# Grouping the output products of a recurrence, and letting TensorE run empty at four weight tiles

## The chip, the cores and the metric

The kernel runs on one core of a Trainium2 chip. The metric is device time in microseconds (us) of one execution; the kernel before takes 1694.59 us, the median of three runs (1694.12 to 1694.8).

## The reference

The input is a sequence of 256 tokens of width 1024. It goes through two blocks. The first has four residual steps: an attention, a squared-ReLU MLP, a gated linear recurrence and another MLP. The second, on which the change acts, puts 16 learned tokens ahead and has one mixer and one expert layer:

```
z = rmsnorm(h, g_mix) @ w_in
conv_val, conv_gate, rwkv_in, gate_logits = jnp.split(z, IN_SPLITS, axis=-1)
y_a = conformer_conv(conv_val, conv_gate, ...)     # 31 taps per channel, 512 channels
y_b = rwkv7_mix(rwkv_in, ...)                      # 8 heads of 64, a state S of 64 x 64 each
h = h + (gate_a * y_a + gate_b * y_b) @ w_o
h = h + peer_ffn(rmsnorm(h, g_ffn), w_q, sub_keys, expert_u, expert_v)
return rmsnorm(h, g_final)[:, N_META:]
```

The recurrence of `rwkv7_mix` is, token by token, `sa = S kk`, `S = S * w - sa (kk * a) + v k`, `o = S r`. `peer_ffn` picks for each token and each of 8 heads 16 of 16384 experts (the best sums of two lists of 128 keys), and gives the sum of gate x GELU(x · u[e]) x v[e] over the 128 chosen experts e.

## The kernel before, in words

**Weights and products.** Every weight tile is 128x1024 in float32 (512 KB). The class `Stream` (L67) loads it on SyncE's queue (`wraw`, L98), ScalarE rounds it to fp32r (`whi`, L121) and VectorE subtracts that from it (`wlo`, L122). A product with such a weight is three products of 256 columns: high by high, high by low, low by high. `mm_T` (L387, products in L392 to L394) runs over the eight 128-row parts of a tile and adds up in one PSUM bank; `mm_blk` (L406, L412 to L414) runs the eight blocks of a tile into four banks, which `product` (L416) holds over all of its tiles. TensorE, shown as PE, takes its weights through a load of their own (PEld) ahead of each product.

**The recurrence.** The 272 tokens are cut into five chunks (c = 0 to 4), the first with the 16 learned tokens. `inverse(c)` (L1117) finds the inverse of a triangular 64x64 matrix per head in steps: VectorE transposes and masks, TensorE multiplies (`p`, `px`, through `mm_heads`, L1115: eight 64x64 products, four head pairs hp times the two halves e of the array, a half being 64 rows and 64 columns). `recur(c)` (L1171) then does the chunk: `pG` (L1175) from the state SV, `pSA` from the inverse X and G, SAV as a copy of it by ScalarE and VectorE (L1182, L1183), the next state through `pN` (L1189) and VectorE (L1194, L1195), and for c of 1 and above the chunk's output `po`: for every head pair and half a product of SV with PRB over all 128 rows (L1203) and, added to it, one of SAV with UC over the 64 rows of its half (L1205). ScalarE copies po into oT (L1207). The steps of the next two chunks' inverses are issued between the steps of `recur`. Beside it TensorE works off products of the input projection (`pz`, L916), and VectorE the 30 taps of the convolution (`cy`, L1230, 120 operations).

**The expert layer.** `peer` (L1344) computes the keys' scores, and then goes over 128 U tiles (L1557): one `mm_T` each into `pu`, the GELU by ScalarE (L1561), and to DRAM. In tiles 0 to 59 VectorE chooses the experts beside it (`select`, L1446; its steps are tied to the GELU of three tiles before), in 60 to 127 `gates` (L1520) builds the gates with short bf16 products on TensorE (`pG`, L1538). Then come 128 V tiles in one `product` (L1615): VectorE multiplies gate and activation (`c`, L1551), the result is split, and the products `yp` of L412 to L414 add up over all tiles; the last three are held back and finished bank by bank.

**Order.** The Tile framework's scheduler puts each engine's instructions in order by its own estimate of when they can start, from the order of the code and its dependences; `tc.issue_after` holds an instruction behind another. On each engine they then run in that order. PSUM tiles of `bank` (L223) rotate over four banks, those of `ybank` are named.

Of the kernel before, what the change touches and what calls it, by code (L numbers as in the profile page):

```python
# [2 lines left out]

# [1 line left out]

# [8 lines left out]
BF16 = mybir.dt.bfloat16  # L14
# [178 lines left out]
def fused_kernel(ctx, tc, A, out, dbg=None, stop=None, start2=False):  # L193
    nc = tc.nc
# [28 lines left out]
    def bank(name, shape=(128, 512)):  # L223
        return ps.tile(list(shape), F32, name=name, tag="g")
# [47 lines left out]
    st = Stream(nc, wraw_p, whl_p, tiles, ahead=2, raw_ahead=2, plain=PLAIN)  # L272
# [33 lines left out]
    TOK = slice(0, T)  # L306
# [80 lines left out]
    def mm_T(p, w, blk, nk, x_hi, x_lo, cs):  # L387

        hi, lo = w
        for k in range(nk):  # L390
            s = slice((blk * nk + k) * 128, (blk * nk + k + 1) * 128)
            nc.tensor.matmul(p, hi[:, s], x_hi[:, k, cs], start=(k == 0), stop=False)  # L392
            nc.tensor.matmul(p, hi[:, s], x_lo[:, k, cs], start=False, stop=False)  # L393
            nc.tensor.matmul(p, lo[:, s], x_hi[:, k, cs], start=False, stop=(k == nk - 1))  # L394

    def mm_T2(nk, x_hi, x_lo, cs, *pw):

# [8 lines left out]
    def mm_blk(ys, blk, w, a_hi, a_lo, first, last):  # L406

        hi, lo = w
        y = ys[blk // 2][:, blk % 2]
        s = slice(blk * 128, (blk + 1) * 128)  # L410
        kw = dict(skip_group_check=True)
        nc.tensor.matmul(y, hi[:, s], a_hi, start=(first and blk % 2 == 0), stop=False, **kw)  # L412
        nc.tensor.matmul(y, hi[:, s], a_lo, start=False, stop=False, **kw)  # L413
        nc.tensor.matmul(y, lo[:, s], a_hi, start=False, stop=last, **kw)  # L414

    def product(n, operand, finish, name, hold=3):  # L416


        ys = ybanks(name)
        held = []  # L420
        for k in range(n):
            if k == n - hold:
                st.pause(hold)
            w, a_hi, a_lo = operand(k)
            if k < n - hold:
                for blk in range(8):
                    mm_blk(ys, blk, w, a_hi, a_lo, k == 0, False)
            else:
                held.append((w, a_hi, a_lo))
        for b in range(4):  # L430
            for i, (w, a_hi, a_lo) in enumerate(held):
                for blk in (2 * b, 2 * b + 1):
                    mm_blk(ys, blk, w, a_hi, a_lo, n == hold and i == 0, i == hold - 1)
            last = finish(b, ys[b])
        return last
# [418 lines left out]
    def mixers(gg, h2, es, setup, after):  # L854
# [10 lines left out]
        with ExitStack() as e2:  # L865
            nk = pool(e2, "mx_n")
# [13 lines left out]
            for tt in range(2):  # L880
                nc.tensor.matmul(pcol[:, tt], row[:, tt * 128:(tt + 1) * 128], ident[0:2, 0:2],
                                 start=True, stop=True)
# [46 lines left out]
        cs = ap.tile([128, 4, 5, 65], F32, name="cs")  # L929
# [37 lines left out]
        for hp in range(4):  # L967
            s = slice(hp * 128, (hp + 1) * 128)
# [18 lines left out]
        PRB = [o2.tile([128, 5, 4, 2, 64], F32, name=f"PRB{e}") for e in range(2)]  # L987
# [28 lines left out]
        for hp in range(4):  # L1016
# [7 lines left out]
            for e in range(2):  # L1024
                r = slice(64 * e, 64 * e + 64)
# [5 lines left out]
        for hp in range(4):  # L1031
# [3 lines left out]
            for e in range(2):  # L1035
                r = slice(64 * e, 64 * e + 64)
# [18 lines left out]
        for j in range(4):  # L1055
            sgs = wk.tile([128, NT], F32, name="sgc", tag="zd")
            p = bank("pz", (128, NT))
            mm_F(p, 4 + j, ALLT)
            nc.scalar.activation(sgs, p, AF.Sigmoid)
            p = bank("pz", (128, NT))  # L1060
# [6 lines left out]
        for c in range(5):  # L1067
            pab = [ybank(e, f"pab{e}", (128, 4, 128)) for e in range(2)]
            for hp in range(4):
                for e in range(2):  # L1070
                    r = slice(64 * e, 64 * e + 64)
                    nc.tensor.matmul(pab[e][:, hp], QK[r, c, hp].rearrange("p a b -> p (a b)"),
                                     PRB[e][r, c, hp].rearrange("p a b -> p (a b)"),
                                     start=True, stop=True)
            for e in range(2):
                for half in range(2):
                    r = slice(64 * half, 64 * half + 64)
# [20 lines left out]
        SV = [bp.tile([128, 5, 4, 64], F32, name=f"SV{e}") for e in range(2)]  # L1098
# [7 lines left out]
        def rb(name, shape):  # L1106
            rot[0] += 1
            return ybank(rot[0] % 4, name, shape)

        HALF = [slice(0, 64), slice(64, 128)]  # L1110
# [60 lines left out]
        def recur(c):  # L1171
            pG = rb("pG", (128, 4, 64))
            for hp in range(4):
                for e in range(2):
                    nc.tensor.matmul(pG[HALF[e], hp], PRB[e][:, c, hp, 0, :], SV[e][:, c, hp],  # L1175
                                     start=True, stop=True)
            G = wk.tile([128, 4, 64], F32, name="G")
            nc.scalar.activation(G, pG, AF.Copy)
            yield
            pS = rb("pSA", (128, 4, 64))  # L1180
            mm_heads(pS, lambda r, hp: X[r, c, hp], lambda r, hp: G[r, hp])
            nc.scalar.activation(SAV[0][0:64, c], pS[0:64], AF.Copy)  # L1182
            nc.vector.tensor_copy(SAV[1][64:128, c], pS[64:128])  # L1183
            yield
            if c < 4:
                pN = rb("pN", (128, 4, 64))
                for hp in range(4):
                    for e in range(2):
                        nc.tensor.matmul(pN[HALF[e], hp], QN[:, c, hp, 64 * e:64 * e + 64],  # L1189
                                         SAV[e][:, c, hp], start=True, stop=True)  # L1190
                for e in range(2):
                    r = HALF[e]
                    t = wk.tile([128, 4, 64], F32, name="Sn")
                    nc.vector.tensor_tensor(t[r], SV[e][r, c], pN[r], op=ALU.add)  # L1194
                    nc.vector.tensor_tensor(SV[e][r, c + 1], t[r],  # L1195
                                            wc[r, :, c:c + 1].to_broadcast([64, 4, 64]),
                                            op=ALU.mult)
            if c >= 1:
                po = rb("po", (128, 4, 64))
                for hp in range(4):  # L1200
                    for e in range(2):
                        r = HALF[e]
                        nc.tensor.matmul(po[r, hp], SV[e][:, c, hp], PRB[e][:, c, hp, 1, :],  # L1203
                                         start=True, stop=False, skip_group_check=True)
                        nc.tensor.matmul(po[r, hp], SAV[e][r, c, hp], UC[r, c, hp, 1, :],  # L1205
                                         start=False, stop=True, skip_group_check=True)
                nc.scalar.activation(oT[:, :, (c - 1) * 64:c * 64], po, AF.Copy)  # L1207
            yield
# [10 lines left out]
        for c in range(5):  # L1219
# [3 lines left out]
            r = recur(c)  # L1223
# [23 lines left out]
        for tt in range(2):  # L1247
            for j in range(4):
                nc.tensor.matmul(pvr[:, 2 * tt:2 * tt + 2], sqc[:, j, tt * 128:(tt + 1) * 128],
                                 ones, start=(tt == 0 and j == 0), stop=(j == 3),  # L1250
                                 skip_group_check=True)
# [4 lines left out]
        for tt in range(2):  # L1256
            nc.tensor.matmul(prd[:, tt * 128:(tt + 1) * 128],
                             rsd[:, tt:tt + 1].to_broadcast([128, 128]), ident,
                             start=True, stop=True)
        nc.vector.tensor_tensor(cy, cy, prd[:, None, :].to_broadcast([128, 4, T]), op=ALU.mult)  # L1260
        a_hi = fp.tile([128, 4, T], F32R, name="a_hi")
        a_lo = fp.tile([128, 4, T], F32R, name="a_lo")
# [21 lines left out]
        for tt in range(2):  # L1284
            s = slice(tt * 128, (tt + 1) * 128)
# [23 lines left out]
        for b in range(16):  # L1309
            if b == GN_AT:  # L1310
                grouped()
            p = bank("pz", (128, T))
# [9 lines left out]
        for i in range(4):  # L1322
            w = st.get(("w_co", i))
            for b in range(2):
                p = bank("pya", (128, T))
                mm_T(p, w, b, 4, a_hi, a_lo, TOK)
                blk = 2 * i + b
                nc.vector.tensor_tensor(sm[:, blk], gates[:, blk], p, op=ALU.mult)
        for i in range(4):
            w = st.get(("w_ro", i))  # L1330
            for b in range(2):
                p = bank("pyb", (128, T))
                mm_T(p, w, b, 4, b_hi, b_lo, TOK)
                blk = 2 * i + b
# [3 lines left out]
        after = product(8, lambda k: (st.get(("w_o2", k)), s_hi[:, k], s_lo[:, k]),  # L1338
                        then_h(col("g_ffn", 0, 8), h2, REAL), "yw")
# [4 lines left out]
    def peer(h2, after):  # L1344
# [5 lines left out]
        rp = pool(es, "pe_r", side="right")  # L1350
# [6 lines left out]

        iorep = rp.tile([128, 128, 2], BF16, name="iorep")
        nc.vector.tensor_copy(iorep, iota[:, :, None].to_broadcast([128, 128, 2]))
        p_hi = rp.tile([128, DC, T], F32R, name="p_hi")  # L1360
        p_lo = rp.tile([128, DC, T], F32R, name="p_lo")

# [20 lines left out]
        for hc in range(18):  # L1383
            if hc < 16:
                if hc < 4:
                    p = pw[hc][0]
# [169 lines left out]
        acts = []  # L1556
        for i in range(128):  # L1557
            p = bank("pu", (128, T))
            mm_T(p, st.get(("u", i)), 0, 8, p_hi, p_lo, TOK)
            hs = h_out[(i // 2) % 4]  # L1560
            acts.append(nc.scalar.activation(hs[:, i % 2], p, AF.Gelu))  # L1561
            if i % 2:
                nc.scalar.dma_start(H[i // 2], hs)
            if ge is not None and c0 is None and next(ge, "done") == "done":
                eu.close()
                cw = pool(es, "pe_c", 3, side="right")
                c0 = combine(0)
            for _ in range(STEPS[i % len(STEPS)]):
                if ge is not None:
                    continue  # L1570
                if i >= U_LAG:
                    with tc.issue_after(acts[i - U_LAG].ins):
                        r = next(se, "done")
                else:
                    r = next(se, "done")
                if r == "done":
                    st.less(PE_MORE)
                    st.less_raw(PE_RAW)
                    ez.close()
                    eh.close()  # L1580
                    G = pool(es, "pe_l").tile([128, 128, T], F32, name="G")
                    ge = gates(G)
                    assert i == U_TOP
# [28 lines left out]
            if b >= 1:  # L1612
                add_sums(b - 1)

        product(128, operand, fin, "yp")  # L1615
        add_sums(3)
        ms = cw.tile([128, 2], F32, name="ms")
        nc.vector.tensor_scalar(ms, psum[:, 0:4:2], 1.0 / D, EPS, op0=ALU.mult, op1=ALU.add)
# [125 lines left out]
```

## Time and profile before

| | |
|---|---|
| median of three runs | 1694.59 us (1694.12 to 1694.8) |
| the profiled execution, its time | 1702.62 us |
| its span | 1700.9 us |
| TensorE products, busy | 1669.2 us (98% of the span) |
| VectorE busy | 1244.0 us (73%) |
| ScalarE busy | 861.3 us (51%) |
| GpSimd busy | 29.8 us (2%) |
| mean granted TensorE clock | 0.986 of full speed |

The span is the time from the first to the last instruction of the profiled execution. A busy TensorE means that products are in flight, not that they follow one another as closely as they can: products overlap, and so their mean duration is longer than the distance between their starts. The stages that matter here stand in this order in the span: the recurrence at about 690 to 778 us, the expert layer's U tiles at about 882 to 1318, its V tiles at about 1318 to 1682.

### The profile page before, as it was taken

How to read it: one execution, taken by the hardware profiler on the slowest of the kernel's cores; microseconds unless marked ns; L12 is line 12 of the kernel's file. 1: busy time of each engine (PE TensorE's matmuls, PEld its weight loads, DVE VectorE, ACT ScalarE, POOL GpSimd, SP SyncE). 2: the span in 40 equal slices, each digit the busy share in tenths (PEclk: the TensorE clock that was granted, in tenths of full speed). 3: DMA queues.
4: the chain of work that ended last, by engine and by line, in shares of the span. 5: the costliest groups of instructions: out<-in, count | busy, mean ns of one | idle time of the engine just before them, and what ended most of it. 6: DMA issues, size and time to landing. Idle time of an engine off the chain costs nothing.

```text
span 1700.9 us, 35211 instructions
## 1 busy us (share of the span) xinstructions
PE 1669.2 (98%) x14458; PEld 1598.2 (94%) x14458; DVE 1244.0 (73%) x2204; ACT 861.3 (51%) x1400; POOL 29.8 (2%) x76
## 2 busy tenths in 40 slices
PE   8999999999999999999999999999999999999997
PEld 7889999899999978778999999999999999999997
DVE  6767555889555688776789984977777777777774
ACT  7555545586544463214465445655555544444443
POOL 0000000011000000001000000000000000000000
PEclk9999999999999999899999999999999999999999
DMA  8426666446665223113664778555555877777773
GB/s 292 135 87 211 188 196 212 136 122 227 199 192 181 74 87 112 39 39 112 211 220 153 217 245 271 173 186 186 185 182 185 298 235 231 236 231 236 229 224 110
DMA packets 96227, 309.75 MB, mean 182 GB/s; under 512 B 12593, under 2 KB 12721, under 8 KB 95681
## 3 DMA queue, kind: packets, MB, share of 16 engines
q1 hardware_dynamic: 83808, 287.61, 53.5%
q10 hardware_dynamic: 11904, 18.25, 2.9%
q8 instruction: 113, 1.85, 0.4%
q0 software_dynamic: 352, 1.64, 0.3%
q14 instruction: 50, 0.40, 0.1%
HBM read 288.58 MB, written 18.87 MB: 181 GB/s over the span
## 4 chain that ended last, share of the span: by engine, by line
PE 87%; DVE 7%; ACT 2%; DMA 2%; issue 1%; POOL 0%; DVEq 0%; SPq 0%; POOLq 0%; ACTq 0%
PE pu L392 10%; PE pu L394 10%; PE pu L393 10%; PE yp L414 7%; PE yp L412 7%; PE yp L413 7%; PE pz L916 4%; PE ym L413 3%; PE ym L414 3%; PE ym L412 3%; PE pG L1538 3%; DVE wlo L122 2%; PE yv L495 1%; ACT whi L121 1%; DVE cy L1230 1%
## 5 line engine op out<-in xcount | busy, mean ns | idle before, releaser
L121 ACT ACTIVATE whi<-wraw 128x1024 fp32r<-128x1024 f32 (+1 forms) x501 | 520.5, 1042 | 549.3 <-PE yp L413 174.2
L122 DVE TENSOR_TENSOR wlo<-wraw,whi 128x1024 fp32r<-128x1024 f32 (+1 forms) x501 | 600.0, 1204 | 254.3 <-ACT whi L121 253.5
L392 PE MATMUL pu<-p_hi,whi 128*128 128x256 f32 x1024 | 292.3, 285 | 0.0
L413 PE MATMUL yp<-p_lo,whi 128*128 128x256 f32 x1024 | 287.8, 281 | 0.0
L412 PE MATMUL yp<-p_hi,whi 128*128 128x256 f32 x1024 | 287.8, 281 | 0.0
L414 PE MATMUL yp<-p_hi,wlo 128*128 128x256 f32 x1024 | 287.6, 281 | 0.1
L394 PE MATMUL pu<-p_hi,wlo 128*128 128x256 f32 x1024 | 286.6, 280 | 0.1
L393 PE MATMUL pu<-p_lo,whi 128*128 128x256 f32 x1024 | 286.7, 280 | 0.0
L413 PEld LDWEIGHTS yp<-p_lo,whi 128*128 128x128 f32 x1024 | 196.5, 192 | 0.0
L393 PEld LDWEIGHTS pu<-p_lo,whi 128*128 128x128 f32 x1024 | 194.5, 190 | 0.0
L394 PEld LDWEIGHTS pu<-p_hi,wlo 128*128 128x128 f32 x1024 | 193.2, 189 | 0.3 <-DVE wlo L122 0.3
L414 PEld LDWEIGHTS yp<-p_hi,wlo 128*128 128x128 f32 x1024 | 192.2, 188 | 0.3 <-DVE wlo L122 0.3
L392 PEld LDWEIGHTS pu<-p_hi,whi 128*128 128x128 f32 x1024 | 192.2, 188 | 0.2 <-ACT xT L1561 0.2
L412 PEld LDWEIGHTS yp<-p_hi,whi 128*128 128x128 f32 x1024 | 192.2, 188 | 0.0
L413 PE MATMUL ym<-s_lo,whi 128*128 128x256 f32 x512 | 142.3, 278 | 1.7 <-DVE s_lo L326 1.6
L412 PE MATMUL ym<-s_hi,whi 128*128 128x256 f32 x512 | 142.4, 278 | 0.5 <-ACT s_hi L325 0.5
L414 PE MATMUL ym<-s_hi,wlo 128*128 128x256 f32 x512 | 142.0, 277 | 0.0
L392 PE MATMUL pu<-h_hi,whi 128*128 128x256 f32 x480 | 133.6, 278 | 0.0
L394 PE MATMUL pu<-h_hi,wlo 128*128 128x256 f32 x480 | 133.2, 277 | 0.2 <-DVE wlo L122 0.2
L393 PE MATMUL pu<-h_lo,whi 128*128 128x256 f32 x480 | 133.1, 277 | 0.0
L413 PEld LDWEIGHTS ym<-s_lo,whi 128*128 128x128 f32 x512 | 96.7, 189 | 2.3 <-DVE s_lo L326 2.3
L412 PEld LDWEIGHTS ym<-s_hi,whi 128*128 128x128 f32 x512 | 96.1, 188 | 0.9 <-ACT s_hi L325 0.7
(479 smaller groups left out, 3317.0 us busy)
## 6 DMA issues: line engine op xcount, KB each, us to landing
wraw<-in_w_dram SPq DMA_DIRECT2D x128, 512.0 KB, 3.6
wraw<-in_u_dram SPq DMA_DIRECT2D x128, 512.0 KB, 3.5
wraw<-in_v_dram SPq DMA_DIRECT2D x128, 512.0 KB, 4.2
wraw<-in_w_in_dram SPq DMA_DIRECT2D x38, 512.0 KB, 3.5
H<-xT ACTq DMA_DIRECT2D x64, 256.0 KB, 2.7
hl<-H SPq DMA_DIRECT2D x64, 256.0 KB, 4.3
wraw<-in_w_qk_dram SPq DMA_DIRECT2D x16, 512.0 KB, 4.3
wraw<-in_rg_in_dram SPq DMA_DIRECT2D x16, 512.0 KB, 5.2
```

The source lines that it names most:

```text
L121: nc.scalar.activation(hi[:, s], t[:, s], AF.Copy)
L122: nc.vector.tensor_tensor(lo[:, s], t[:, s], hi[:, s].bitcast(F32), op=ALU.subtract)
L392: nc.tensor.matmul(p, hi[:, s], x_hi[:, k, cs], start=(k == 0), stop=False)
L393: nc.tensor.matmul(p, hi[:, s], x_lo[:, k, cs], start=False, stop=False)
L394: nc.tensor.matmul(p, lo[:, s], x_hi[:, k, cs], start=False, stop=(k == nk - 1))
L412: nc.tensor.matmul(y, hi[:, s], a_hi, start=(first and blk % 2 == 0), stop=False, **kw)
L413: nc.tensor.matmul(y, hi[:, s], a_lo, start=False, stop=False, **kw)
L414: nc.tensor.matmul(y, lo[:, s], a_hi, start=False, stop=last, **kw)
L495: nc.tensor.matmul(yv[2 * tt + h], a[:, dc, s], w[:, h * 512:(h + 1) * 512], start=(dc == 0 and a is h_hi and w is hi), stop=(dc == 7 and ...
L916: nc.tensor.matmul(p, w[:, k * 128:(k + 1) * 128], h_f[:, k, cs], start=(k == 0), stop=(k == DC - 1))
L1230: nc.vector.scalar_tensor_tensor(cy[:, j], cu[:, j, tap:tap + T], col("conv_w", tap * 4 + j), cy[:, j], op0=ALU.mult, op1=ALU.add)
L1538: nc.tensor.matmul(p[:, t], eq[:, 0, b, :, e], ob[:, b, k, :, e], start=(k == 0), stop=(k == 2))
```

## The change

1. In `recur`, po's eight products of SV come first, with the two halves of the array in turn, and only then the eight of SAV, again with the halves in turn. The bank is started by the first product of each half alone (`hp == 0`).
2. A new helper, `drain`: a 2x2 bf16 product of a small tile `kd`, a GpSimd memset of `kd`, and a second 2x2 product of it, which has to wait for the memset, as the memset has to wait for the first product. The products that follow are issued behind the second. So TensorE has nothing in flight while GpSimd works.
3. It is called ahead of the U tiles 2 and 16 and of the V tiles 3 and 40. `kd` is made, and set to zero, at the start of `peer`.

```
+            last = nc.tensor.matmul(p, lo[:, s], x_hi[:, k, cs], start=False, stop=(k == nk - 1))
+        return last
...
+        return nc.tensor.matmul(y, lo[:, s], a_hi, start=False, stop=last, **kw)
...
+    def drain(kd, after):
+        p = bank("drain", (2, 2))
+        with tc.issue_after(after.ins):
+            nc.tensor.matmul(p, kd[:, 0:2], kd[:, 2:4], start=True, stop=True)
+        nc.gpsimd.memset(kd, 0.0)
+        with tc.issue_after(after.ins):
+            last = nc.tensor.matmul(p, kd[:, 0:2], kd[:, 2:4], start=True, stop=True)
+        return tc.issue_after(last.ins)
...
             if k < n - hold:
-                for blk in range(8):
-                    mm_blk(ys, blk, w, a_hi, a_lo, k == 0, False)
+                with drain(kd, mm) if k in drains else nullcontext():
+                    for blk in range(8):
+                        mm = mm_blk(ys, blk, w, a_hi, a_lo, k == 0, False)
...
             if c >= 1:
                 po = rb("po", (128, 4, 64))
+                for hp in range(4):
+                    for e in range(2):
+                        nc.tensor.matmul(po[HALF[e], hp], SV[e][:, c, hp], PRB[e][:, c, hp, 1, :],
+                                         start=(hp == 0), stop=False, skip_group_check=True)
                 for hp in range(4):
                     for e in range(2):
                         r = HALF[e]
-                        nc.tensor.matmul(po[r, hp], SV[e][:, c, hp], PRB[e][:, c, hp, 1, :],
-                                         start=True, stop=False, skip_group_check=True)
                         nc.tensor.matmul(po[r, hp], SAV[e][r, c, hp], UC[r, c, hp, 1, :],
                                          start=False, stop=True, skip_group_check=True)
...
+        kd = rp.tile([128, 4], BF16, name="kd")
+        nc.gpsimd.memset(kd, 0.0)
...
-            mm_T(p, st.get(("u", i)), 0, 8, p_hi, p_lo, TOK)
+            w = st.get(("u", i))
+            with drain(kd, mm) if i in (2, 16) else nullcontext():
+                mm = mm_T(p, w, 0, 8, p_hi, p_lo, TOK)
...
-        product(128, operand, fin, "yp")
+        product(128, operand, fin, "yp", drains=(3, 40), kd=kd)
```

The change moves instructions on TensorE. In the chunk c = 3, before, each SV product (SV_8057 is the half e = 0, SV_8058 the half e = 1) is followed by the SAV product of the same half:

```order
L1115 MATMUL px<-X,T_8738 64x64 x8
L1203 MATMUL po<-PRB_7472,SV_8057 64x64
L1205 MATMUL po<-UC,SAV_8059 64x64
L1203 MATMUL po<-PRB_7473,SV_8058 64x64
L1205 MATMUL po<-UC,SAV_8060 64x64
```

After, in the same place:

```order
L1127 MATMUL px<-X,T_8738 64x64 x8
L1215 MATMUL po<-PRB_7472,SV_8057 64x64
L1215 MATMUL po<-PRB_7473,SV_8058 64x64
...
L1215 MATMUL po<-PRB_7473,SV_8058 64x64
L1220 MATMUL po<-UC,SAV_8059 64x64
L1220 MATMUL po<-UC,SAV_8060 64x64
```

All eight SV products now stand ahead of the eight SAV products, and in each group the halves alternate; what stands ahead of po and behind it is the same.

In the last chunk, c = 4, where there is no next state, po before (its SAV products wait for pSA, which stands between them):

```order
L1156 MATMUL px<-X,T_8818 32x32 x7
L1203 MATMUL po<-PRB_7472,SV_8057 64x64
L916 MATMUL pz<-h_f,wraw_9146 128x256
L1115 MATMUL pSA<-G,X 64x64 x8
L916 MATMUL pz<-h_f,wraw_9146 128x256 x3
L1205 MATMUL po<-UC,SAV_8059 64x64
L1203 MATMUL po<-PRB_7473,SV_8058 64x64
```

After, in the same place (the numbers of lines have moved by 12 to 15):

```order
L1168 MATMUL px<-X,T_8818 32x32 x7
L1215 MATMUL po<-PRB_7472,SV_8057 64x64
...
L1127 MATMUL pSA<-G,X 64x64
L1215 MATMUL po<-PRB_7473,SV_8058 64x64
L1127 MATMUL pSA<-G,X 64x64 x7
L1215 MATMUL po<-PRB_7472,SV_8057 64x64
L1215 MATMUL po<-PRB_7473,SV_8058 64x64
L928 MATMUL pz<-h_f,wraw_9146 128x256
L1220 MATMUL po<-UC,SAV_8059 64x64
L928 MATMUL pz<-h_f,wraw_9146 128x256
L1220 MATMUL po<-UC,SAV_8060 64x64
```

The SV products now stand ahead of pSA and among its products, the SAV products together behind it, with products of the input projection (pz) between.

Between the V tiles 2 (whi_16428) and 3 (whi_16462), before:

```order
L412 MATMUL yp_16423<-p_hi,whi_16428 128x256
L413 MATMUL yp_16423<-p_lo,whi_16428 128x256
L414 MATMUL yp_16423<-p_hi,wlo_16429 128x256
L412 MATMUL yp_16420<-p_hi,whi_16462 128x256
L413 MATMUL yp_16420<-p_lo,whi_16462 128x256
L414 MATMUL yp_16420<-p_hi,wlo_16463 128x256
```

After, in the same place (the same tiles are whi_16438 and whi_16472):

```order
L413 MATMUL yp_16433<-p_hi,whi_16438 128x256
L414 MATMUL yp_16433<-p_lo,whi_16438 128x256
L415 MATMUL yp_16433<-p_hi,wlo_16439 128x256
L421 LDWEIGHTS kd
L421 MATMUL drain<-kd 2x2
L424 LDWEIGHTS kd
L424 MATMUL drain<-kd 2x2
L413 MATMUL yp_16430<-p_hi,whi_16472 128x256
L414 MATMUL yp_16430<-p_lo,whi_16472 128x256
L415 MATMUL yp_16430<-p_hi,wlo_16473 128x256
```

Two weight loads and two 2x2 products stand between the last product of tile 2 and the first of tile 3. The other three drains look the same. On GpSimd four memsets come in, one per drain, and one where kd is made. On VectorE and ScalarE only a few instructions change places with a neighbour, on SyncE none.

## Rows read from the trace of the kernel before

**Rows 1.** The page, busy time by engine, and the chain by engine.

```profile
PE 1669.2 (98%) x14458; PEld 1598.2 (94%) x14458; DVE 1244.0 (73%) x2204; ACT 861.3 (51%) x1400; POOL 29.8 (2%) x76
...
PE 87%; DVE 7%; ACT 2%; DMA 2%; issue 1%; POOL 0%; DVEq 0%; SPq 0%; POOLq 0%; ACTq 0%
```

**Rows 2.** Windows: us, busy (instructions) of PE, PEld, DVE, ACT, POOL, PEclk, DMA share, GB/s.

```profile
727.00:776.00 49.00, 49.00 (x702) 36.99 (x702) 37.44 (x95) 10.36 (x29) 0.00 (x0) 1.00 0.15 41
780.00:800.00 20.00, 19.48 (x125) 16.85 (x124) 12.25 (x23) 11.23 (x26) 0.99 (x1) 0.89 0.24 81
882.00:1003.00 121.00, 121.00 (x1027) 120.67 (x1025) 121.00 (x447) 59.23 (x91) 0.00 (x0) 1.00 0.63 197
1000.00:1020.00 20.00, 19.92 (x170) 19.52 (x168) 14.28 (x20) 10.54 (x16) 0.00 (x0) 1.00 0.83 280
1030.00:1060.00 30.00, 30.00 (x267) 30.00 (x266) 13.56 (x12) 14.62 (x22) 0.00 (x0) 1.00 0.81 256
1340.00:1660.00 320.00, 320.00 (x2719) 320.00 (x2719) 226.15 (x343) 155.76 (x228) 0.00 (x0) 1.00 0.74 236
```

**Rows 3.** The chain of waits through 727 to 776 us, by line.

```profile
by line: PE pz L916 33.7%; PE po L1205 14.5%; PE po L1203 13.5%; PE px L1115 11.6%; PE p L1115 9.5%; PE pN L1189 4.3%; PE pG L1175 3.8%; PE pSA L1115 3.2%; PE px L1156 2.8%; PE p L1148 2.3%; PE pz L392 0.9%; PE pz L393 0.2%
```

**Rows 4.** Waits in 1320 to 1660 us: us in total, times, longest.

```profile
ACT whi L121 <- PE yp L413: 161.3, 112, 1.5
```

**Rows 5.** Products by line in 143:158, 1004:1010.5, 1013:1079, 1103:1316, 1319:1681, 1682.5:1684.2; busy, mean ns.

```profile
L413 PE MATMUL ym<-s_lo,whi 128*128 128x256 f32 x22 | 6.1, 276 | 0.0
L392 PE MATMUL pu<-p_hi,whi 128*128 128x256 f32 x19 | 5.3, 281 | 0.0
L392 PE MATMUL pu<-p_hi,whi 128*128 128x256 f32 x195 | 53.8, 276 | 0.0
L393 PE MATMUL pu<-p_lo,whi 128*128 128x256 f32 x477 | 134.0, 281 | 0.0
L412 PE MATMUL yp<-p_hi,whi 128*128 128x256 f32 x1004 | 282.1, 281 | 0.0
L412 PE MATMUL yp<-p_hi,whi 128*128 128x256 f32 x5 | 1.4, 277 | 0.0
```

**Rows 6.** Timeline of PEld and PE: start, us, instruction, in brackets idle and releaser.

```profile
1003.09 0.19 PEld L394 LDWEIGHTS pu<-p_hi,wlo 128*128 128x128 f32 x1 [0.28 <-DVE wlo L122]
...
1011.32 0.28 PE L394 MATMUL pu<-p_hi,wlo 128*128 128x256 f32 x1
...
1011.59 0.19 PEld L392 LDWEIGHTS pu<-p_hi,whi 128*128 128x128 f32 x1 [0.20 <-ACT xT L1561]
...
1011.82 0.28 PE L393 MATMUL pu<-p_lo,whi 128*128 128x256 f32 x1
```

**Rows 7.** Timeline of PE, 758.7 to 767.2 us.

```profile
758.74 0.68 PE L1115 MATMUL px<-X,T 64*64 64x64 f32 x16
759.35 0.33 PE L1203 MATMUL po<-PRB,SV 128*64 128x64 f32 x2
759.61 0.33 PE L1205 MATMUL po<-UC,SAV 64*64 64x64 f32 x2
...
763.46 0.70 PE L916 MATMUL pz<-h_f,wraw 128*128 128x256 f32 x2
...
766.37 0.69 PE L1175 MATMUL pG<-SV,PRB 128*64 128x64 f32 x16
766.98 0.48 PE L916 MATMUL pz<-h_f,wraw 128*128 128x256 f32 x1
```

**Rows 8.** Waits in 720 to 784 us.

```profile
DVE T L1133 <- PE p L1115: 8.1, 6, 3.0
```

**Rows 9.** Timeline at GpSimd's power operation, 784.5 to 789 us.

```profile
786.72 0.99 POOL L359 TENSOR_TENSOR rstd<-var,mhalf 128x2 f32<-128x2 f32 x1 [146.59 <-DVE var L1253]
787.76 0.73 PEld L1257 LDWEIGHTS prd<-ident,rstd 128*128 128x128 f32 x4 [0.92 <-POOL rstd L359]
```

**Rows 10.** Groups by line on POOL.

```profile
L821 POOL MEMSET sel<- 64x1 f32 x8 | 0.8, 96 | 0.3
```

More of the change, by code (lines that the diff above doesn't have):

```diff
@@ L1 @@
 import math
-from contextlib import ExitStack
+from contextlib import ExitStack, nullcontext
 import numpy as np
@@ L393, in mm_T @@
             nc.tensor.matmul(p, hi[:, s], x_lo[:, k, cs], start=False, stop=False)
-            nc.tensor.matmul(p, lo[:, s], x_hi[:, k, cs], start=False, stop=(k == nk - 1))
+            last = nc.tensor.matmul(p, lo[:, s], x_hi[:, k, cs], start=False, stop=(k == nk - 1))
+        return last
     def mm_T2(nk, x_hi, x_lo, cs, *pw):
@@ L413, in mm_blk, with product @@
         nc.tensor.matmul(y, hi[:, s], a_lo, start=False, stop=False, **kw)
-        nc.tensor.matmul(y, lo[:, s], a_hi, start=False, stop=last, **kw)
-    def product(n, operand, finish, name, hold=3):
+        return nc.tensor.matmul(y, lo[:, s], a_hi, start=False, stop=last, **kw)
[7 more added lines that the diff above has]
+        return tc.issue_after(last.ins)
+    def product(n, operand, finish, name, hold=3, drains=(), kd=None):
         ys = ybanks(name)
```

## The prediction

> **What bounds the kernel now.** I read the page first. TensorE is busy for 98% of the span, and the chain that ended last runs through it for 87% [rows 1]. So a gain must come from TensorE's own work, and the busy share alone does not say whether that work goes as fast as it could.
>
> Next the windows of the three stretches that the change touches [rows 2]. In the recurrence (727 to 776 us) TensorE is busy for all of the 49.00 us and VectorE for 37.44; every step of the chain there is TensorE's, 28% of it po [rows 3]. In the early U tiles (882 to 1003) VectorE is busy for 121.00 of 121 us: TensorE looks full there, but whoever takes time off it finds VectorE as the bound. In the V tiles (1340 to 1660) TensorE alone is full: VectorE 226 of 320 us, the DMA share 0.74. ScalarE's splits of V weights wait 161.3 us for TensorE to give tiles back [rows 4], so the supply has room.
>
> Then the same instruction in different stretches. The 128x256 products of the weight loops have two paces with equal shapes and a granted clock of 1.00. In V 320.00 us hold 2719 records, two of them cut by the window's edges: 320/2717 = 117.8 ns from one to the next. At 1030 to 1060 it is 30/265 = 113.2 [rows 2]. The mean durations go with it: 281 ns against 276 [rows 5]. The difference is 4.5 ns of a product, and V has 3072 products.
>
> Last the timeline, for where the pace changes. It does not drift: it changes only where TensorE ran empty or took small products in between, and then holds. At 1003.09 the weights of a U tile came late (0.28 us idle) and the loop went on at 281; at 1011.59 it stood again, for 0.20 us behind a GELU, and from 1012 it ran at 276 [rows 5, 6]. I count nine stops within product loops, from 141.98 to 1682.30 us, that are followed by a run of equal products: after six of them the pace is the fast one (the stretches behind the first and the last are in [rows 5]), after three the slow one. During the gates (1103 to 1316), where each U tile comes after a group of short bf16 products, all 60 tiles are slow [rows 5].
>
> **The recurrence's output products.** Per chunk, before: sixteen products (8 SV, 8 SAV), an SV and an SAV in turn, two records each; from 759.35 to 763.46 that is 4.11 us, 0.257 a product [rows 7]. An SV product takes all 128 rows, the SAV product behind it 64 rows in the same half of the columns. After: eight SV products with the halves in turn, then eight SAV products with the halves in turn. Both forms stand in the trace beside it: eight 64x64 products with halves in turn took 758.74 to 759.35, 0.61 us, and eight 128x64 products with halves in turn (pG) took 766.37 to 766.98, again 0.61 [rows 7]. So 4.11 becomes 1.22, 2.9 less, and four chunks give −11.6 at most. In the last chunks the SV round can start before SAV is there, but the SAV round still waits for pSA and ScalarE, so I count 2.3, 2.7, 2.9 and 2.0 for chunks 1 to 4: 9.9.
>
> The Trainium skill speaks against half of this ("TensorE: Matmul & The Clock Gate", section "The mechanism"): a weight load overlaps running products only where it goes to other rows of the array. SV's loads take all rows, so by that rule the SV round would keep its 0.257 us a product and the saving would be 1.4 a chunk. pG, whose products also take all rows, disagrees with 0.61 us for eight [rows 7].
>
> VectorE bounds it from the other side: of the 49 us it is idle 11.6, and 8.1 of the waits (T behind the products p, in 720 to 784) are waits for TensorE [rows 2, 8]. The waits that stay (hops between engines, the first operation after each product) come to 2 to 2.5 us, an estimate from the many waits of 0.3 us that view has; so the stretch shrinks by 9.4 at most. I take −9.0. Ends: −6.5 if the convolution's VectorE operations land between the steps of the inverse, −10.5 if all that I counted comes through.
>
> **The drains.** Each adds two pairs of weight load and 2x2 product, one GpSimd memset and two hops between engines, with TensorE waiting; everything behind it on TensorE waits, the other engines run on. No row shows such a round trip. From below: the cheapest stop and restart is 1011.32 to 1011.82, 0.50 us where two products take 0.24, so 0.26 [rows 6]. From above: a GpSimd operation of 0.99 us that TensorE waited for kept its weight load idle for 0.92 [rows 9], with about 0.7 for emptying, hops and restart: 1.6. A memset of GpSimd takes 96 ns [rows 10], far less than the 0.99. I estimate 0.28 (the last product runs out) + 0.10 (memset) + 0.15 (hops) + 0.26 (restart) − 0.12 (the place of one product) = 0.7, rounded up to 0.75. Four drains: 3.0, between 1.0 and 6.4.
>
> In V two drains cost 1.5 in full, since TensorE is the bound. If the stretch behind each runs at the fast pace, tiles 3 to 39 (37 x 24 = 888 products) and tiles 40 to 124 (85 x 24 = 2040) give 2928 x 4.5 ns = 13.2. V then asks for weights 4% sooner; at 256 GB/s the stretch 1030 to 1060 was fed at the fast pace [rows 2]. V: −11.7.
>
> In U the drains stand at tiles 2 and 16, within the stretch where VectorE is the bound [rows 2]. A faster TensorE only comes sooner to weights that are not split yet; a drain's cost is covered by the distance that VectorE's splits are ahead, which shrinks to nothing at 1003.09 [rows 6]. What they may change is the pace after the last stop: 1012 to 1085 is fast now, and 644 products turned slow would cost 2.9. I take +0.8, half of the price of two drains, with −0.3 and +4 as ends. The gates' 60 tiles are reset to the slow pace by their bf16 products, so no drain reaches them.
>
> The memset when kd is made, and the PSUM tile of a drain (one of four that rotate), cost nothing: GpSimd is busy for 2% of the span [rows 1]; if the rotation did make TensorE wait for a GELU, it would be some 0.2 us a drain as at 1011.59 [rows 6].
>
> Sum: −9.0 − 11.7 + 0.8 = −19.9. It is made in an execution of 1702.62 us (span 1700.9), 8.0 longer than the median of 1694.59; I take differences over to the median: 1674.7.
>
> **Rivals.** *One V stretch stays slow.* The drain ends in a short bf16 product, as the gates' groups do, and three of nine stops ended slow. If the drain at tile 3 fails, V has −9.2 + 1.5 = −7.7 and the time is 1678.7; if the one at tile 40 fails, −4.0 + 1.5 = −2.5 and 1683.9.
>
> *The drains only cost.* All 60 tiles behind bf16 products are slow [rows 5], and if it is these that set the pace, every drain sets the slow one: −9.0 + 3.0, 1688.6; against it, nine such stops have shown both. The Trainium skill has no second pace at all: the same page, section "Back-to-back issue gap", gives the gap at full clock by the number of columns alone, 109 ns for 256 columns, and by it nothing would be gained in V. The trace differs: 113.2 and 117.8 at one clock and one shape [rows 2].
>
> *Nothing is left of it.* VectorE eats most of the recurrence's gain (−5), or a phase of the granted clock shifts against it, while the drains cost 3 to 5: 1692 to 1696. For it: VectorE's 37 of 49 us. Against it: it would need both.
>
> *Slower: the clock falls at every drain.* At 780 to 800, where TensorE waits for the GpSimd operation, the mean granted clock is 0.89 [rows 2], 2.2 us of full speed lost. If each drain did that, it would cost 0.75 + 2.2 = 2.95, four 11.8; with −6.5 from the recurrence that gives +5.3, 1699.9. It decides from some 2.5 us a drain. Against it: 1000 to 1020 has two stops within 9 us and a clock of 1.00 [rows 2].
>
> **How the numbers follow.** Forecast (recurrence and both V drains) 0.48; one V stretch slow 0.20; drains only cost 0.22; nothing left 0.06; slower 0.04. The forecast's own range is 1671 to 1678: recurrence −6.5 to −10.5, drains at 0.26 to 1.6, U up to +4, not all at once. The likeliest time is 1674.7. Holding eight times in ten, the range reaches over the one-drain cases and the drains-only case, from 1671 to 1690; beyond it lie the last two cases and the tails. What this measurement can tell from no change is 0.2%, 3.4 us. Faster: the first three cases but for the upper tail of the third, 0.90; same: that tail and the fourth, 0.06; slower 0.04.
>
> **What would show it.** Right: po as two groups of about 0.6 us a chunk, and the stretch 727 to 776 about 9 us shorter with VectorE nearer to full; V products at 276 ns and 113 apart from tile 3 on; TensorE's idle at each drain 0.3 to 1.6 us; the U stretch up to its end at nearly its old length. Wrong: po's products still 0.257 us each, or faster with VectorE's splits and TensorE's waits growing by the same; V at 281 after the drains; a granted clock below 1.00 at a drain; or V's weights late at the fast pace, with TensorE waiting for VectorE's splits.

## The result, and the profile after

The change takes 1669.46 us, the median of four runs (1667.99 to 1671.14), beside 1694.36 for the kernel before (four runs): a ratio of 0.9855, interval 0.9837 to 0.9872. It is faster by 24.9 us. Forecast were 19.9 us less, 1674.7; the time lies 1.5 us below the range's lower end of 1671.

In the experiments below, executions of one kernel spread by up to 28 us (before: 1681.6 to 1709.3), and most of that goes with the granted clock. The profile gives it per stretch. First rows of the kernel before that were not shown yet: windows, with us, busy times of PE, PEld, DVE, ACT and POOL, PEclk, DMA share and GB/s.

```profile
670.00:700.00 30.00, 30.00 (x148) 23.32 (x148) 17.04 (x33) 8.65 (x24) 0.00 (x0) 0.60 0.06 18
709.50:778.57 69.07, 69.07 (x993) 51.64 (x990) 53.84 (x135) 13.99 (x40) 0.00 (x0) 0.99 0.17 48
770.00:840.00 70.00, 69.48 (x520) 62.59 (x519) 49.91 (x100) 35.34 (x67) 5.14 (x4) 0.93 0.50 162
```

The same stretches of the kernel after, by the work in them (the recurrence starts 12 us sooner), and two of V:

```profile
670.00:700.00 30.00, 29.87 (x347) 23.26 (x345) 27.22 (x61) 9.42 (x26) 0.00 (x0) 1.00 0.12 37
697.60:756.38 58.78, 58.58 (x993) 44.51 (x990) 51.67 (x132) 13.90 (x40) 0.00 (x0) 1.00 0.15 47
760.00:830.00 70.00, 69.04 (x551) 64.84 (x550) 50.61 (x95) 38.37 (x67) 5.26 (x5) 0.98 0.59 188
1318.00:1412.00 94.00, 94.00 (x832) 94.00 (x831) 69.66 (x107) 48.06 (x71) 0.00 (x0) 1.00 0.77 254
1420.00:1640.00 220.00, 220.00 (x1943) 220.00 (x1943) 158.66 (x239) 110.07 (x160) 0.00 (x0) 1.00 0.72 236
```

Line by line. Ahead of the recurrence, in work that the change does not touch, the profiled execution of before ran at a mean clock of 0.60 for 30 us (12 us lost), that of after at 1.00. The recurrence, from the first pG to pm (the mean over the convolution's output, the first product behind the last chunk), is 69.07 us before and 58.78 after, with the same 993 product records; 0.4 of the 69.07 are half clock at its end, from 777.8 us on. Behind it before lost 70 x 0.07 = 5 us to half clock, after 1.7. In V 220/1941 = 113.3 ns lie between two products, 117.8 before [rows 2].

po after, timeline of PE in the chunk that [rows 7] shows of before (start, us, instruction):

```profile
741.78 0.68 PE L1127 MATMUL px<-X,T 64*64 64x64 f32 x16
742.39 0.69 PE L1215 MATMUL po<-PRB,SV 128*64 128x64 f32 x16
743.01 0.68 PE L1220 MATMUL po<-UC,SAV 64*64 64x64 f32 x16
743.62 0.70 PE L928 MATMUL pz<-h_f,wraw 128*128 128x256 f32 x2
```

4.11 us have become 1.23. The drain ahead of V tile 3, timeline of PE and, in the middle, of POOL:

```profile
1313.04 0.28 PE L415 MATMUL yp<-p_hi,wlo 128*128 128x256 f32 x1
1313.25 0.17 PE L421 MATMUL drain<-kd 128*2 128x2 bf16 x1
...
1313.54 0.10 POOL L422 MEMSET kd<- 128x4 bf16 x1 [375.39 <-PE drain L421]
...
1313.69 0.16 PE L424 MATMUL drain<-kd 128*2 128x2 bf16 x1 [0.28 <-POOL kd L422]
1313.79 0.39 PE L413 MATMUL yp<-p_hi,whi 128*128 128x256 f32 x1
1314.01 0.28 PE L414 MATMUL yp<-p_lo,whi 128*128 128x256 f32 x1
```

From 1313.04 to 1314.01 are 0.97 us where two products took 0.24: a drain costs 0.73. The products by line that answer to [rows 5], in 999 to 1059 (U, behind the last stop), 1318 to 1412 and 1420 to 1640 (V):

```profile
L393 PE MATMUL pu<-p_lo,whi 128*128 128x256 f32 x171 | 48.1, 281 | 0.0
L413 PE MATMUL yp<-p_hi,whi 128*128 128x256 f32 x277 | 76.5, 276 | 0.0
L413 PE MATMUL yp<-p_hi,whi 128*128 128x256 f32 x647 | 178.6, 276 | 0.0
```

V is fast behind both drains, and the granted clock is 1.00 from 768 to 1658 us, over all four drains, so the rival in which it falls at every drain is gone. The U stretch that was fast before is slow in this execution.

### The profile page after: what moved, and what is told of

It reads as the page before. It is cut to its first block, busy times and chain, and to the rows that moved or that the text cites. A ratio compares the mean times of both kernels' runs of the same rounds, so it can differ in the third digit from the quotient of the medians.

```text
span 1667.7 us, 35236 instructions
## 1 busy us (share of the span) xinstructions
PE 1632.5 (98%) x14466; PEld 1567.0 (94%) x14466; DVE 1244.2 (75%) x2204; ACT 861.9 (52%) x1400; POOL 32.5 (2%) x81
## 4 chain that ended last, share of the span: by engine, by line
PE 68%; issue 16%; DVE 10%; ACT 3%; DMA 2%; POOL 1%; DVEq 0%; POOLq 0%; SPq 0%; ACTq 0%
PE pu L392 9%; PE pu L394 9%; PE pu L393 9%; PE pz L928 4%; PE ym L414 3%; PE ym L415 3%; PE ym L413 3%; DVE wlo L122 3%; PE pG L1555 3%; PE yp L413 2%; PE yp L414 2%; PE yp L415 2%; PE yv L507 1%; DVE cy L1245 1%; ACT whi L121 1%
## 5 line engine op out<-in xcount | busy, mean ns | idle before, releaser
L413 PE MATMUL yp<-p_hi,whi 128*128 128x256 f32 x1024 | 283.1, 276 | 0.0
L415 PE MATMUL yp<-p_hi,wlo 128*128 128x256 f32 x1024 | 282.8, 276 | 0.1
L414 PE MATMUL yp<-p_lo,whi 128*128 128x256 f32 x1024 | 282.9, 276 | 0.0
L414 PEld LDWEIGHTS yp<-p_lo,whi 128*128 128x128 f32 x1024 | 192.3, 188 | 0.0
```

The source lines that it names most:

```text
L415: return nc.tensor.matmul(y, lo[:, s], a_hi, start=False, stop=last, **kw)
```

## The experiments

Time alone cannot tell these kernels apart, because of the clock, so each is read in two ways: the median of its runs, and parts of its trace, measured between instructions that all kernels have. "Like executions" are those with a mean granted clock above 0.988, which shuts out the long half-clock stretch ahead of the recurrence. Of the kernel before, 42 of the 69 timed beside the experiments are such, median 1691.7; of the change 6 of 10, median 1669.7. They come from three chips, on which the like executions of before have medians of 1691.3, 1693.3 and 1692.6; differences of 1 to 2 us between versions say nothing.

**The recurrence edit alone.** The kernel before with

```
-  for hp, e: SV product (start=True), SAV product
+  for hp, e: SV product (start=(hp == 0));  then for hp, e: SAV product
```

> The recurrence edit alone, without drains. Theory A (the edit shortens the recurrence by what the grouped products save, 10.3 us between the first pG and pm in the trace of the change; what is beyond that between the two profiles is half clock in the one execution of before that was profiled, 682 to 706 us on the clock's own axis, upstream of the edit): 1683 to 1685 us, 10 us below before. Theory B (the edit itself brings the 22 us that lie between the two profiles at pm, the clock included): 1671 to 1674 us. Theory C (the prediction's term, 9.0): 1685.4.

1680.28 (ratio 0.9941, interval 0.9909 to 0.9972; like executions 1680.1, so −11.6). From the first pG to pm (timeline of PE) it is 58.75 us, as in the change:

```profile
696.92 0.39 PE L1175 MATMUL pG<-SV,PRB 128*64 128x64 f32 x6
...
755.67 0.38 PE L1245 MATMUL pm<-cy,omean 128*128 128x256 f32 x1
```

V stays slow, as it should without drains (products in 1320 to 1640):

```profile
L412 PE MATMUL yp<-p_hi,whi 128*128 128x256 f32 x907 | 254.9, 281 | 0.0
```

Theory B falls by its time, but A's 1683 to 1685 and C's 1685.4 were missed as well, from the other side: −11.6 (−11.2 against the 24 like executions of before on the same chip) is more than 10.3. Time less what half clock took (span times one minus the mean clock) is 1669.8 on average (standard error 0.8) against 1677.7 (0.5) for before on that chip, −7.9 with a standard error of 0.9: so the surplus goes with half clock (below).

**The drains alone.** The change with the old po.

> The four drains alone, the recurrence as before. Theory A (V 11.5 us shorter by the pace of 113 ns, U 2.8 us longer): 1685.7 us, V products at 276 ns from tile 3 on. Rival (drains only cost, the V stretch would have been at the fast pace for another reason): 1697. If most of the 24.9 us came from the drains: below 1682.

1682.97 (0.9935, 0.9907 to 0.9963; like executions 1682.6, −9.1). V's first 125 tiles take 341.8 us where before, a second execution of it and the recurrence edit alone all take 353.3. Theory A's pace holds, and the rival of 1697 falls; A's 2.8 us longer U was not seen (172.0 us here, below), and the time is lower than its 1685.7 by as much. The two parts add up: −11.6 − 9.1 = −20.7 against −22.0 for both in like executions.

**Without the drains in U.** The change with `i in ()`.

> The change without its two drains in U; the recurrence edit and the V drains stay. Theory A (the U drains cost 2.8 us: their price and, after the last stop at tile 30, the slow pace in tiles 34 to 59): 1666.7 us, and the U products behind the last stop at 276 ns as in before. Rival (the U drains pay for themselves, the stop at tile 30 is what sets the pace behind it and falls as it likes): 1669 to 1671.

1673.83 (0.9903, 0.9861 to 0.9945), which neither theory has. The trace, of an execution of 1670.43 us, shows a part of why: the drain ahead of V tile 3 left the pace slow, and only that at tile 40 turned it, which cost 345.8 − 341.8 = 4.0 us; what the six others did was not profiled. Products in 1316 to 1414 and 1422 to 1640:

```profile
L413 PE MATMUL yp<-p_hi,whi 128*128 128x256 f32 x278 | 78.1, 281 | 0.0
L413 PE MATMUL yp<-p_hi,whi 128*128 128x256 f32 x642 | 177.2, 276 | 0.0
```

For U the traces of all kernels serve: from the first product of U tile 0 to that of tile 61, the five executions without drains there take 170.8 to 174.6 us, mean 172.3, the six with drains at 2 and 16 170.6 to 174.2, mean 172.1. So the U drains neither cost nor give; what differs is how the last stop behind tile 30 ends, fast or slow, with either. Theory A's 2.8 us was that one execution.

**The kernel before, again.** No edit.

> The kernel before, unchanged, for a second profile of it. Theory A (the half clock of 23.9 us ahead of the recurrence is of one execution, not of the kernel): same time, 1694.4 us, and a trace with less half clock in 670 to 700 us and a span nearer to 1692. Rival (it belongs to the kernel before): the same 23.9 us of half clock again.

1696.71 (1.0004, 0.9971 to 1.0037), and its profile has the long half-clock stretch again (13.7 us lost ahead of the recurrence). Theory A's trace was not seen; but the drains alone, with the same code up to there, had none of it in the same place:

```profile
670.00:700.00 30.00, 29.87 (x347) 23.20 (x345) 27.21 (x61) 9.40 (x26) 0.00 (x0) 1.00 0.12 37
740.00:820.00 80.00, 78.54 (x694) 66.98 (x692) 50.91 (x107) 33.23 (x69) 5.26 (x5) 0.94 0.37 119
```

**The change, again.** No edit, beside 17 runs of before.

> The change, unchanged, beside more runs of before on one chip. Theory A (of the 24.9 us some 19 are the change's own work at full clock, recurrence, V and U together, and some 6 a smaller loss to half clock in the executions that were timed): time times granted clock, span less what half clock took, is 18 to 20 us lower than that of before; the medians differ by 20 to 26 as the half-clock stretches fall. Rival (the change also does away with the long half-clock stretch ahead of the recurrence): none of its executions has a clock under 0.989.

1676.65 against 1695.22 (0.9882, 0.9839 to 0.9924): 18.6 us less, where the first measurement had 24.9. Four of its six executions have clocks of 0.984 to 0.988, and its profile shows the stretch:

```profile
670.00:700.00 30.00, 30.00 (x112) 23.28 (x112) 16.16 (x29) 7.18 (x19) 0.00 (x0) 0.54 0.06 18
```

So the rival falls. The five profiles with the long stretch have a mean clock of 0.986 or 0.987, the nine without it 0.992 or more; if 0.988 or less is taken as its sign, it came in 4 of 10 executions of the change and 27 of 69 of before. Over all versions with one edit or both it is 15 of 80, so whether the edits make it rarer stays open. Time less what half clock took is 1657.7 on average (standard error 2.3) against 1679.1 (0.3): −21.4, within its error of A's 18 to 20.

**Drains without the memset.** The edit, and a look at tile 3 and what follows:

```
-        nc.gpsimd.memset(kd, 0.0)
```

> The change with the memset left out of the drain, so that the two 2x2 products stand there and TensorE waits for nothing. Theory A (the stop sets the pace, not the small product): the two products cost some 0.1 us, V stays at 281 ns and 117.8 ns apart, and the time is 10 us above the change, near 1680. Rival (any short foreign product can start the pace anew): V at 276 ns, and the time some 2 us below the change.

1667.02 (0.9833, 0.9794 to 0.9873): theory A falls, and the rival holds. Timeline of PE at V tile 3, and V's products in 1316 to 1410:

```profile
1311.21 0.28 PE L415 MATMUL yp<-p_hi,wlo 128*128 128x256 f32 x1
1311.42 0.17 PE L421 MATMUL drain<-kd 128*2 128x2 bf16 x1
1311.44 0.16 PE L423 MATMUL drain<-kd 128*2 128x2 bf16 x1
1311.54 0.39 PE L413 MATMUL yp<-p_hi,whi 128*128 128x256 f32 x1
1311.76 0.28 PE L414 MATMUL yp<-p_lo,whi 128*128 128x256 f32 x1
```
```profile
L413 PE MATMUL yp<-p_hi,whi 128*128 128x256 f32 x278 | 76.7, 276 | 0.0
```

TensorE never waits for GpSimd, the pair costs 0.55 − 0.24 = 0.31 us, and the pace turns fast all the same. (In U the pair at tile 2 left it slow, that at 16 turned it.)

**V drains at tiles 1 and 4, none in U.** `drains=(1, 4)`, `i in ()`.

> No drains in U, those in V ahead of tiles 1 and 4 instead of 3 and 40. Theory A (a drain turns a slow stretch fast in about five of six cases, and leaves a fast one fast; the second is there for the sixth case): V 0.2 us shorter than in the change and seldom slow to its end, U 2.8 shorter where the stop at tile 30 ends fast: 1666 to 1668 where the change takes 1669.5. Rival (the pace after a drain falls by chance each time, also from a fast stretch): V slow in every third execution, a spread of 13 us.

1672.26 (0.9853, 0.9812 to 0.9893; like executions 1671.9), not below the change. V is fast from tile 1 on (341.6 us for 125 tiles, 0.2 less than the change, as expected), but U took 174.6 here, its last stop having ended slow.

**32 more drains among the gates.** `or (i >= 64 and i % 2 == 0)`.

> The change with 32 more drains, ahead of every second U tile from 64 on, where each tile comes behind bf16 products that leave the slow pace. It measures the price and the odds of a drain. Theory A (price 0.73 us, as the gaps 0.206, 0.442, 0.094 and 0.222 us in the trace of the change give less two products of 0.118; fast afterwards in five of six cases, until the next bf16 products): 32 x 0.73 less 32 x 24 x 4.5 ns at most, 20 to 23 us above the change. Rival (the drain's end, a short bf16 product, leaves the slow pace here as the gates' own do): no tile fast, 23.4 above.

1680.42 (0.9914, 0.9876 to 0.9951). Tile 61 to V's first product takes 246.8 us, 8.8 more than in the change, less than either theory. Products in 1120 to 1310:

```profile
L393 PE MATMUL pu<-p_lo,whi 128*128 128x256 f32 x408 | 112.8, 276 | 0.0
```

Fast throughout, also the tiles between, which have no drain ahead of them. The trace shows what they have instead. Timeline of PE at the drain of tile 64, and the group ahead of tile 65:

```profile
1092.22 0.86 PE L1555 MATMUL pG<-ob,eq 128*128 128x128 bf16 x12
1093.01 0.17 PE L421 MATMUL drain<-kd 128*2 128x2 bf16 x1
1093.11 0.40 PE L1555 MATMUL pG<-ob,eq 128*128 128x128 bf16 x4
1093.46 0.16 PE L424 MATMUL drain<-kd 128*2 128x2 bf16 x1
1096.40 0.63 PE L1555 MATMUL pG<-ob,eq 128*128 128x128 bf16 x8
```

Four of the next group's twelve products of the gates went between the drain's two, and eight were left ahead of tile 65. Over all fourteen traces the pace was slow behind each of 828 whole groups of twelve with no drain or pair behind them (18 came out of a fast tile), and fast behind each of 32 groups of eight (all came out of a fast tile). No run varied that number by itself. The 64 fast tiles give back 64 x 24 x 4.5 ns = 6.9 us; the drains cost 15.7/32 = 0.49 each.

**The version that these runs pointed to.** Pairs without memset at U 35, 62, 64, 66, 80 and V 1, 4, 8.

> The best version the runs so far point to: the recurrence edit, and pairs of 2x2 products without memset or wait ahead of the U tiles 35, 62, 64, 66 and 80 and of the V tiles 1, 4 and 8, none in the early U tiles. Theory A (a small product can turn a slow stretch fast, and a fast one stays fast, also across the gates' bf16 products): U tiles 36 to 127 and V at 113 ns apart; 8 pairs of 0.32 us; the gates' 60 tiles give 60 x 24 x 4.5 ns = 6.5 us: 1658 to 1661 us, and U from tile 61 to V's first product 231 to 232 us where the change has 238.0. Rival (the pace behind a small product falls by chance each time): gates partly slow, time near the 1667 of the run without memsets.

1672.66 (0.9873, 0.9829 to 0.9918; like executions 1671.0): not better than the change, so theory A falls. V is fast (341.1 us). Among the gates the tile right behind each pair is fast and the next, behind a whole group of twelve, slow again; tile 61 to V's first product is 238.7.

**A single 2x2 product for a drain.** Its first product and the memset left out.

> The change with a single 2x2 product in the place of each drain: no memset, no wait, no second product. Theory A (any product of another shape between two of the loop can start the pace anew): V fast from tile 3 or from tile 40, time as without memsets, 1666 to 1668, a product costing about 0.2 us. Rival (it takes the pair, with a second load queued behind a short product): V at 281 ns to its end, some 10 us more, 1677.

1672.77 (0.9862, 0.9823 to 0.9900). V stays slow behind the first and is fast behind the second, so one product is enough but not sure. Products in 1316 to 1412 and 1420 to 1640:

```profile
L413 PE MATMUL yp<-p_hi,whi 128*128 128x256 f32 x272 | 76.4, 281 | 0.0
L413 PE MATMUL yp<-p_hi,whi 128*128 128x256 f32 x647 | 178.6, 276 | 0.0
```

**One drain among the gates.** `i in (2, 16, 64)`.

> The change with one more drain, ahead of U tile 64. Theory A (the pace is a state that the gates' bf16 products keep, slow or fast; the one drain turns it): U tiles 64 to 127 at 276 ns, from tile 61 to V's first product 231.5 us where the change has 238.0; 6 us below the change in like executions. Rival, as the prediction had it (each bf16 group resets the pace to slow): only tile 64 or 65 is fast, 238.5 us.

1668.94 (0.9835, 0.9787 to 0.9883). The rival holds: 238.3 us from tile 61 to V, and the tiles are slow in 1095 to 1300:

```profile
L393 PE MATMUL pu<-p_lo,whi 128*128 128x256 f32 x458 | 128.7, 281 | 0.0
```

Tile 64 behind the drain and tile 65 behind a group of eight are fast; from tile 66, behind the first whole group of twelve, all are slow. So the bf16 products do bring the slow pace back.

**Grouped, but the halves apart.** In both of po's loops:

```
-  for hp in range(4): for e in range(2):
+  for e in range(2): for hp in range(4):
```

> The change with po's products grouped, but the halves not in turn: four SV products of the one half, four of the other, then SAV likewise. Theory A (what saves is that products in turn go to different halves of the array and overlap): po 0.13 to 0.26 us a product again, 2 to 4 us a chunk, and most of the recurrence's 10.3 us gone. Rival (what costs is the change between 128 rows and 64 rows in one half, sixteen times a chunk): po near 1.2 us a chunk, as in the change.

1674.39 (0.9899, 0.9840 to 0.9958). Timeline of PE, the third chunk:

```profile
750.72 0.97 PE L1215 MATMUL po<-PRB,SV 128*64 128x64 f32 x16
751.61 0.96 PE L1220 MATMUL po<-UC,SAV 64*64 64x64 f32 x16
752.51 1.13 PE L928 MATMUL pz<-h_f,wraw 128*128 128x256 f32 x4
```

1.79 us for po: 0.112 us a product in one half, 0.077 with halves in turn, 0.257 with 128 and 64 rows in turn. The change of shape was most of the cost (4.11 to 1.79), the turns are the rest (to 1.23). The recurrence takes 60.81 us, 2.0 more than with halves in turn, and neither theory is whole. One rival no run separates: in the old order each SAV product also adds to the part of PSUM that the product just ahead of it wrote. Against it: the gates' products do that too, three in a row, and stand 56 ns apart (twelve in 0.67 us, 1069.48 to 1070.15 in the trace of the change).

## Why the prediction was right and wrong

**The recurrence was mis-sized: −9.0, measured −11.6 (like executions, the edit alone).** Two steps fail.

The count of the products was right: 9.9 forecast from 4.11 to 1.22 a chunk, 69.07 − 58.78 = 10.3 measured. Without the half clock inside it, the three traces with the old po take 68.6 to 68.7 us there and the ten with the halves in turn 58.8 to 59.2: 9.6 less. The prediction had cut its count by a bound from VectorE, "the stretch shrinks by 9.4 at most", and that step fails, though its number came out near. It took VectorE's idle time from 727 to 776 us, but the steps that can close up fill the whole stretch from the first pG to pm, 709.5 to 778.6. Over that VectorE is idle for 69.07 − 53.84 = 15.2 us, and 7.1 us of that are left after: VectorE never became the bound.

The second, and the larger, is half clock at the end of the recurrence and behind it, which the sum put at nothing. Between 740 and 850 us the three executions profiled with the old po lose 5.1 us each to it; the eleven with a grouped po lose 0 to 3.4, mean 2.2. The prediction saw the dips of before [rows 2] but left them out of the sum. Why a shorter recurrence has fewer of them stays open; no run here varied that alone.

**V was right.** −11.7 forecast, 353.3 − 341.8 = −11.5 measured. The price of a drain was right as well (0.75 against 0.73), with a memset of 0.10; TensorE's idle of 0.28 lies just under the 0.3 to 1.6 that it named. Odds: a drain turned a slow V fast in 8 of 10 cases (in U and among the gates in 8 of 8), a fast V stayed fast in 6 of 6, and without any small product V was slow to its end in 3 of 3. The rival "drains only cost" is gone. So is what the prediction made of the stop: it is not needed. Short products of another shape, without a wait, turned it in 3 of 4 cases (in U and among the gates in 5 of 6), so the wait inside a drain, 0.42 of its 0.73 us, bought nothing that these runs show. The cases are too few to tell these odds apart. The Trainium skill's gaps ("TensorE: Matmul & The Clock Gate", section "Back-to-back issue gap") go by columns alone, and its formula, from which the prediction's 109 ns come, is there for single products, not for a stream of weight loads and products. The trace has both 117.8 and 113.2 at one number of columns. No run here shows what in the array the two paces are.

**U was right in kind:** nothing gained or lost on average (−0.2), +0.8 forecast; what the stop behind tile 30 does falls either way.

**The gates were right:** their bf16 products bring back the slow pace (one drain there changes nothing), each time a whole group of twelve stands ahead of a tile. Drains ahead of every second tile kept it fast, as they split every second group, and cost more than that gave. Not every short group does so: behind three 128-column products (pgt) ahead of tiles 60 and 61 the pace was fast in 28 of 28 cases, four of them out of a slow tile.

**The Trainium skill's rule on weight loads** that spoke against the edit (the same page, section "The mechanism") is not borne out: SV's eight products, all on 128 rows, took 0.62 us with the halves in turn.

**From one profile to the median.** "I take differences over to the median" hides that the profiled execution had 12 us of half clock in 670 to 700 that most executions lack. It did no harm to the sum, whose terms lie elsewhere; but the 33 us between the two profiles would have misled anyone who read the result from them. The 3.4 us that the prediction took as the least that can be told from no change rested on three runs within 0.7 us; later executions spread by 28. In like executions the change is worth −22.0: −11.6 for the recurrence, −9 to −11 for the drains. At full clock the traces' terms, with both V stretches fast, add up to −9.6 − 11.5 − 0.2 = −21.3, 1.4 beyond the forecast; fewer dips of the clock come on top. The first four runs gave −24.9, six later ones −18.6; the forecast of −19.9 lies between them. So the range's lower end was missed by what the recurrence gave beyond its term, most of it the clock, and by which executions were drawn: none of the first four of the change had the long half-clock stretch (clocks of 0.993 to 0.995), which is luck. What the clock did in the four first runs of before was not recorded, so this last part is not shown.

## What to carry to other kernels

Group small products by the rows and columns of the array that they use, and let neighbours in a group go to different halves: the order alone was worth 0.257 against 0.077 us a product. Compare the distance between equal products in different stages; where it differs at one clock, a small product of another shape may set the faster pace, a group of them the slower, and the odds are counted by traces, not by times. Before a bound from another engine cuts a counted gain, take that engine's idle time over the whole stretch that can move. Where the rows show a lower granted clock in or behind the stretch, give it a term of its own.

## What the runs showed of the hardware that was not expected

- One sequence of products has two paces, 117.8 and 113.2 ns, that hold over thousands of products and can change at a pair of 2x2 products that costs 0.31 us. Out of a fast stretch, a group of twelve short bf16 products left the slow one in 18 of 18 cases, a group of eight the fast one in 32 of 32.
- The granted clock can be half for some 24 to 27 us of one execution and full in another one of the same program, in the same place, at a cost of 12 to 14 us; for that reason two profiles can differ by more than the change that they are to show.
